# Attention in a hybrid block: adding the two row halves of a head's output by DMA in DRAM, one low part of k for both heads, and a 65th column in the sum of squares

## The chip, the cores and the metric

The kernel runs on one core of one Trainium2 chip. A core has five engines that each work through a queue of their own in order: TensorE (PE, matmuls; the loads of its stationary operand are shown apart as PEld), VectorE (DVE), ScalarE (ACT), GpSimd (POOL) and SyncE (SP, which only issues transfers). DMA transfers are issued here by SP and by POOL; POOL's go through a queue of their own ("software" in the profile), SP's through another ("hardware").

The metric is the device time of one execution in microseconds (us).

## The reference

One layer of a decoder trunk, sequence 1024, model width 1024, all in float32. The change touches the attention group (8 heads of 64).

```python
hn = rms_norm(h, norm1_g[i])
proj = hn @ w_in[i]
...
q = rms_norm(q.reshape(bsz, s_len, ATTN_HEADS, HEAD_DIM), q_norm_g[i])
k = rms_norm(k.reshape(bsz, s_len, ATTN_HEADS, HEAD_DIM), k_norm_g[i])
...
y_b = stick_breaking_attention(q, k, v).reshape(bsz, s_len, ATTN_W)
...
h = h + jnp.concatenate([y_a, y_b, y_c], axis=-1) @ w_out[i]
f = jnp.square(jax.nn.relu(rms_norm(h, norm2_g[i]) @ w_ff1[i]))
h = h + f @ w_ff2[i]
gate = jax.nn.sigmoid(rms_norm(h, norm3_g[i]) @ w_ple_gate[i])
h = h + gate * (p[i] @ w_ple_proj[i])
```

```python
def stick_breaking_attention(q, k, v):          # per block of 128 queries
    z = jnp.einsum('bqhd,bkhd->bhqk', qi, kj) * scale
    causal = s_pos < t_pos
    log_beta = jax.nn.log_sigmoid(z)
    log_rem = jnp.where(causal, jax.nn.log_sigmoid(-z), 0.0)
    suffix = lax.cumsum(log_rem, axis=3, reverse=True) - log_rem
    weights = jnp.where(causal, jnp.exp(log_beta + suffix), 0.0)
    o = jnp.einsum('bhqk,bkhd->bqhd', weights, vj)
```

## The kernel before

**Precision.** A float32 operand is kept as two rounded parts, hi and lo; a product is three matmuls, hi*hi, hi*lo and lo*hi (`product`, L157 to L163). `split` (L131 to L139) makes the two parts: hi on ACT, lo on DVE.

**The stages.** First the input, its norm and two small projections. Then, from about 60 us, the spatial gating and `project(0)`. Then the attention of four pairs of heads: `attend(pr)` is woven on PE with `project(pr + 1)`, which makes q, k and v of the next pair; beside `attend(3)` stands `convolve` (`weave`, a count of units of work decides whose turn it is). Then the output projection w_out, the squared-ReLU MLP (two thirds of the time, done as a seven-product block scheme), and the gate at the end.

**project(pr)** loads eight weight blocks `w_qkv` (`load_w`: an SP transfer into one of 7 `stage` buffers, hi on ACT, lo on DVE, or on POOL for the even ones). For each of eight blocks of 128 tokens, 24 matmuls fill the bank `qkv_ps` (one of two). Then a chain follows: ACT squares q and k into `qk_sq` (L335), DVE sums 64 columns for each of four heads (L337), DVE scales the sums and adds the epsilon, which here depends on the token (`ms1e[t]`, L339), POOL takes the power -1/2 (`rs`, L169), DVE multiplies (L345), and V is split. `turn_qk` transposes two blocks at a time and makes `QS` (q's hi and lo, stacked in the 128 partitions) and `KH` (k's hi twice). k's low part has a tile for each head and half of the sequence: `KL[hh][th]`, whose own 64 partitions DVE writes (L370, two instructions of 64 partitions) and whose other 64 POOL sets to zero (L323).

**attend(pr)** does eight steps, head 0 with g = 0 to 3, head 1 with g = 3 to 0, g a block of 256 queries. `stick` makes z (L402: k's hi against q's hi and lo; L404: k's low part, 128 partitions of which 64 are zero; L408: the mask), two sigmoids on ACT (L409, L410), a scan on DVE (L413) and a product on POOL or DVE (L416). `gather` transposes the weights (`w_tr`), splits them into `wT_hi` and `wT_lo`, and multiplies with V, hi in 64 columns and lo in the other 64, so that the bank `av` holds two row halves whose sum is the output. ACT copies one half to `av_lo` (L462), DVE adds it to the other (L463) into `y_b`, and SP stores `y_b` to `y_dram` once per half of the sequence (L466). `av_lo` and `qk_sq` share one pool of three buffers (`half_tmp`, L79).

**POOL's other work in this stretch** is `block_sums` (L282 to L300): before each `gather` it issues up to two transfers of 1 MB that build sums of blocks of `w_ff2` in DRAM (`w_sums`), by plain copies (L300) and by copies that add to what stands there (L297).

**The order.** The program is written in this order, but a scheduler decides what stands where in each engine's queue. On the chip each queue is worked through in that fixed order.

Of the kernel before, what the change touches and what calls it, by code (L numbers as in the profile page):

```python
# [7 lines left out]
F32 = mybir.dt.float32  # L8
F32R = mybir.dt.float32r
AF = mybir.ActivationFunctionType  # L10
ALU = mybir.AluOpType
AX = mybir.AxisListType

P = 128
# [4 lines left out]
HD = 64  # L19
PLE = 256  # L20
FT = 16
EPS = 1e-6
STAGES = 7
WBUFS = 20
SLOTS = 56
LATE = {"w": 22, "raw": 4, "sum": 6, "tmp": 12, "R": 2}
# [6 lines left out]
def hybrid_block(ctx: ExitStack, tc: tile.TileContext, a: dict):  # L33
# [5 lines left out]
    nc = tc.nc  # L39
# [9 lines left out]
    tp = front.enter_context(tc.tile_pool(name="tp", bufs=6))  # L49
# [7 lines left out]
    def name(s):  # L57
        n_of[0] += 1
        return f"{s}_{n_of[0]}"

    def slot(s, dt=F32, shape=(P, HT)):
        return sp.tile(list(shape), dt, tag="slot", name=name(s))
# [10 lines left out]
    def halves(s, dt=F32, shape=(P, HT)):  # L73
        return [slot(s, dt, shape) for _ in range(2)]
# [1 line left out]
    def tmp(s, dt=F32, shape=(P, HT)):  # L76
        return tp.tile(list(shape), dt, tag="tmp", name=name(s))

    def half_tmp(s, dt=F32):  # L79
        return tp.tile([P, 256], dt, tag="half", name=name(s), bufs=3)  # L80

    def bank(pool, s):
        return pool.tile([P, HT], F32, tag=pool.name, name=name(s))
# [9 lines left out]
    half = [slice(0, HT), slice(HT, T)]  # L93
# [34 lines left out]
    gk = load_const("gk", [P, 1])  # L128


    def split(src, hi, lo, scale=None, low=nc.vector):  # L131

        if scale is None:
            nc.scalar.copy(hi, src)  # L134
            low.tensor_tensor(out=lo, in0=src, in1=hi, op=ALU.subtract)  # L135
        else:
            nc.scalar.activation(hi, src, AF.Copy, scale=scale)
            nc.vector.scalar_tensor_tensor(out=lo, in0=src, scalar=scale, in1=hi,  # L138
                                           op0=ALU.mult, op1=ALU.subtract)  # L139
# [70 lines left out]
    ms1e, r1, r1h = [], [], []  # L210
# [20 lines left out]
    lo_p, hi_p = slice(0, HD), slice(HD, P)  # L231
# [72 lines left out]
    y_dram = dram.tile([6, 2, P, HT], F32, name="y_dram")  # L304

    def project(pr):

        wk = [load_w(a["w_qkv"][pr, k], 384, nc.gpsimd if pr and k % 2 == 0 else nc.vector)
              for k in range(KT)]

        QS = [[None, None], [None, None]]

        KH = [[None, None], [None, None]]
        KL = [[None, None], [None, None]]
        V = [None] * 4
        low_q = [None, None]
        heads[pr] = QS, KH, KL, V, low_q
        for t in range(KT):
            th, ts = block(t)
            if t % 4 == 0:  # L320
                for hh, other in enumerate((hi_p, lo_p)):
                    KL[hh][th] = slot("KL", F32R)
                    nc.gpsimd.memset(KL[hh][th][other].bitcast(F32), 0.0)  # L323
                KH[0][th] = slot("KH", F32R)
                QS[0][th] = slot("QS", F32R)
                low_q[th] = slot("q_lo", F32R)
                QS[1][th] = slot("QS", F32R)
                KH[1][th] = slot("KH", F32R)
            ps = bank(ps_mm, "qkv_ps")[:, :384]
            for k0 in range(0, KT, 2):  # L330
                product(ps, [(cols(xn[k][th], ts), wk[k]) for k in (k0, k0 + 1)],
                        k0 == 0, k0 == KT - 2)
                yield 18
            sq = half_tmp("qk_sq")
            nc.scalar.activation(sq, ps[:, :256], AF.Square)  # L335
            ss = small.tile([P, 4], F32, tag="ss", name=name("ss"))
            nc.vector.tensor_reduce(out=ss, in_=sq.rearrange("p (h d) -> p h d", d=HD),  # L337
                                    axis=AX.X, op=ALU.add)
            nc.vector.tensor_scalar(out=ss, in0=ss, scalar1=1.0 / HD, scalar2=ms1e[t],  # L339
                                    op0=ALU.mult, op1=ALU.add)  # L340
            rs = small.tile([P, 4], F32, tag="rs", name=name("rs"))
            power_mhalf(rs, ss, 4)
            if t % 2 == 0:
                qk = tp.tile([P, 2, 256], F32, tag="qk", name=name("qk"), bufs=2)
            nc.vector.tensor_tensor(  # L345
                out=qk[:, t % 2].rearrange("p (h d) -> p h d", d=HD),
                in0=ps[:, :256].rearrange("p (h d) -> p h d", d=HD),
                in1=rs.unsqueeze(2).broadcast_to([P, 4, HD]), op=ALU.mult)
            if t % 2 == 0:
                V[t // 2] = slot("V", F32R, (P, 2, 2, 2, HD))  # L350
            v = V[t // 2][:, t % 2]
            split(ps[:, 256:].rearrange("p (h d) -> p h d", d=HD), v[:, :, 0], v[:, :, 1], scale=r1[t])
            if t % 2 == 1:
                later(72, lambda t=t, qk=qk: turn_qk(heads[pr], t, qk))

    def turn_qk(head, t, qk):

        QS, KH, KL, _, low_q = head
        th = t // 4
        tr = bank(ps_tr, "qk_tr")  # L360
        for i in range(2):
            for j in range(2):
                o = j * 256 + i * P
                nc.tensor.transpose(tr[:, o:o + P], qk[:, i, j * P:(j + 1) * P], ident)
        ws = slice((t % 4 - 1) * P, (t % 4 + 1) * P)

        split(tr[:, :256], QS[0][th][:, ws], low_q[th][:, ws], scale=gq)
        nc.scalar.activation(KH[0][th][:, ws], tr[:, 256:], AF.Copy, scale=gk)
        for hh, own in enumerate((lo_p, hi_p)):
            nc.vector.scalar_tensor_tensor(out=KL[hh][th][own, ws], in0=tr[own, 256:],  # L370
                                           scalar=gk[own], in1=KH[0][th][own, ws],
                                           op0=ALU.mult, op1=ALU.subtract)
        if t % 4 == 3:
            nc.scalar.copy(KH[1][th][hi_p], KH[0][th][hi_p])
            nc.scalar.copy(KH[1][th][lo_p], KH[0][th][hi_p])
            nc.scalar.copy(KH[0][th][hi_p], KH[0][th][lo_p])
            nc.vector.tensor_copy(QS[1][th][hi_p], QS[0][th][hi_p])
            nc.vector.tensor_copy(QS[1][th][lo_p], low_q[th][hi_p])
            nc.vector.tensor_copy(QS[0][th][hi_p], low_q[th][lo_p])
        return 8  # L380
# [3 lines left out]
    def attend(pr):  # L384

        QS, KH, KL, V, _ = heads[pr]
        yb = halves("y_b")
        weights = {}

        def stick(hh, g):  # L390
            weights[hh, g] = []
            for t in (2 * g, 2 * g + 1):
                W = (t + 1) * P
                th, ts = block(t)

                rem = at.tile([P, T], F32, tag="rem", name=name("rem"), bufs=3)
                wt = at.tile([P, T], F32, tag="wt", name=name("wt"), bufs=4)
                for kh in reversed(range(th + 1)):
                    n = min(HT, W - kh * HT)
                    ks = slice(kh * HT, kh * HT + n)  # L400
                    z = bank(ps_z, "z")[:, :n]
                    nc.tensor.matmul(z, QS[hh][th][:, ts], KH[hh][kh][:, :n],  # L402
                                     start=True, stop=False)
                    nc.tensor.matmul(z, QS[hh][th][:, ts], KL[hh][kh][:, :n],  # L404
                                     start=False, stop=kh < th)
                    if kh == th:

                        nc.tensor.matmul(z[:, n - P:], ident_r, below, start=False, stop=True)  # L408
                    nc.scalar.activation(rem[:, ks], z, AF.Sigmoid, scale=-HD ** -0.5)  # L409
                    nc.scalar.activation(wt[:, ks], z, AF.Sigmoid, scale=HD ** -0.5)  # L410

                back = rem[:, :W][:, ::-1]
                nc.vector.tensor_tensor_scan(out=back, data0=back, data1=back, initial=1.0,  # L413
                                             op0=ALU.mult, op1=ALU.bypass)
                on_vector = t in (3, 5, 7)
                done = (nc.vector if on_vector else nc.gpsimd).tensor_tensor(  # L416
                    out=wt[:, :W - 1], in0=wt[:, :W - 1], in1=rem[:, 1:W], op=ALU.mult)
                if not on_vector:
                    last_pool[0] = done
                weights[hh, g].append(wt)  # L420
                yield 2 * (t + 1) + 10

        def gather(hh, g):
# [21 lines left out]
            for j in range(-2, g + 1):  # L445
# [12 lines left out]
                                         stop=kb == 2 * g + 1 and part is lo)  # L458
                yield 8

            low = half_tmp("av_lo")
            nc.scalar.copy(low[:HD], av[HD:])  # L462
            nc.vector.tensor_tensor(out=yb[g // 2][own, (g % 2) * 256:(g % 2 + 1) * 256],  # L463
# [6 lines left out]
        for i, step in enumerate(steps):  # L470
            if i + 1 < len(steps):
                yield from stick(*steps[i + 1])
            block_sums(8 * pr + i, last_pool[0])
            yield from gather(*step)

    ATTEND = 2 * (72 + 8 * 10 + 72 + 10 * 10 + 80)

# [619 lines left out]
```

## Time and profile before

| | |
|---|---|
| median of 3 runs | 1260.59 us (1258.04 to 1261.03) |
| profiled execution | 1262.6 us, of it 1260.9 us from the first to the last instruction (the span) |
| busy: PE, DVE, ACT, POOL | 96%, 70%, 48%, 29% of the span |
| mean granted TensorE clock | 0.984 of full speed |
| transfers: hardware queue, software queue | 168.08 MB, 65.70 MB |

In the rows below a group reads: line, engine, operation, output <- inputs, shapes, count, then busy time and mean duration of one, then the idle time of the engine just before them and who ended it. A timeline row is start, duration, engine, line, operation, tiles and count. A window row has the length of the stretch, then the busy time and the count of instructions for each engine, then the granted clock, the share of the time in which the DMA engines were busy, and GB/s.

### The profile page before, as it was taken

The page shows a single profiled execution, that of the slowest core. Times are in us where ns is not written, and L with a number is a line of the kernel's source. Part 1 is how long each engine was busy: PE and PEld are TensorE (multiplying, and loading weights), DVE is VectorE, ACT ScalarE, POOL GpSimd, SP SyncE. Part 2 cuts the span into 40 slices and gives each one's busy share as a digit, 9 for nine tenths or more (in the row PEclk, how much of TensorE's full clock was granted, in tenths as well). Part 3 has the DMA queues.
Part 4 walks back from the last instruction along what each step waited for, and adds up shares of the span by engine and source line. Part 5 has one row for each costly group of instructions (what it writes and reads, how often), then busy time and mean ns, then how long its engine had stood idle before and what let it go on. Part 6 is the DMA issues. An engine that isn't in the chain of part 4 may idle for free.

```text
span 1260.9 us, 17509 instructions
## 1 busy us (share of the span) xinstructions
PE 1215.0 (96%) x5868; PEld 1034.1 (82%) x5868; DVE 880.7 (70%) x1324; ACT 603.8 (48%) x1167; POOL 364.2 (29%) x365
## 2 busy tenths in 40 slices
PE   9999898899999999879999999999999999999998
PEld 7898798898888878658888888888888888888887
DVE  7746886898979654676887777777755565686443
ACT  7725655666656454553334334344544344555211
POOL 2324434455323212233553453431000000122110
PEclk9999998999999999989999999999999999999999
DMA  9603257788542298689999999958956565653231
GB/s 309 211 18 117 84 158 210 167 210 159 119 114 38 67 292 226 175 221 251 269 244 255 252 244 250 252 193 302 354 179 224 183 223 170 203 166 106 76 111 51
DMA packets 118700, 234.89 MB, mean 186 GB/s; under 512 B 13105, under 2 KB 20529, under 8 KB 118353
## 3 DMA queue, kind: packets, MB, share of 16 engines
q1 hardware_dynamic: 94752, 168.08, 40.4%
q0 software_dynamic: 23856, 65.70, 23.3%
q8 instruction: 46, 0.75, 0.3%
q14 instruction: 46, 0.37, 0.1%
HBM read 176.57 MB, written 78.64 MB: 202 GB/s over the span
## 4 chain that ended last, share of the span: by engine, by line
PE 82%; DVE 8%; DMA 5%; issue 2%; ACT 1%; POOL 1%; SPq 0%; DVEq 0%; POOLq 0%; ACTq 0%
PE d_ps L731 24%; PE f_ps L731 24%; PE qkv_ps L161 3%; PE qkv_ps L162 3%; PE qkv_ps L163 3%; PE g_ps L161 2%; PE g_ps L163 2%; PE g_ps L162 2%; DVE rem L413 2%; PE av L456 2%; DMA S<-sq 2%; PE w_tr L438 1%; PE cv_ps L161 1%; DMA h_dram<-h 1%; PE cv_ps L162 1%
## 5 line engine op out<-in xcount | busy, mean ns | idle before, releaser
L135 DVE TENSOR_TENSOR w_lo<-raw,w_hi 128x512 fp32r<-128x512 f32 x268 | 244.9, 916 | 94.4 <-ACT w_hi L134 92.2
L134 ACT CAST w_hi<-raw 128x512 fp32r<-128x512 f32 x268 | 165.2, 619 | 242.6 <-PE d_ps L731 116.7
L731 PE MATMUL f_ps<-hn_hi,w_hi 128*128 128x512 f32 x448 | 176.5, 394 | 5.3 <-ACT v L884 5.3
L731 PE MATMUL f_ps<-hn_lo,w_hi 128*128 128x512 f32 x448 | 175.7, 392 | 0.0
L731 PE MATMUL f_ps<-hn_hi,w_lo 128*128 128x512 f32 x448 | 175.3, 392 | 0.0
L731 PE MATMUL d_ps<-f_hi,w_lo 128*128 128x512 f32 x448 | 174.3, 389 | 0.0
L731 PE MATMUL d_ps<-f_hi,w_hi 128*128 128x512 f32 x448 | 174.3, 389 | 0.0
L731 PE MATMUL d_ps<-f_lo,w_hi 128*128 128x512 f32 x448 | 174.3, 389 | 0.0
L731 PEld LDWEIGHTS f_ps<-hn_hi,w_hi 128*128 128x128 f32 x448 | 85.1, 190 | 23.4 <-ACT v L884 5.7
L719 POOL TENSOR_TENSOR S<-S,sq 128x512 f32<-128x512 f32 x14 | 22.6, 1614 | 273.5 <-ACT sq L788 273.5
L731 PEld LDWEIGHTS f_ps<-hn_lo,w_hi 128*128 128x128 f32 x448 | 85.1, 190 | 17.9 <-issue 0.2
L731 PEld LDWEIGHTS f_ps<-hn_hi,w_lo 128*128 128x128 f32 x448 | 85.0, 190 | 18.0
L731 PEld LDWEIGHTS d_ps<-f_hi,w_hi 128*128 128x128 f32 x448 | 84.1, 188 | 17.6
L731 PEld LDWEIGHTS d_ps<-f_lo,w_hi 128*128 128x128 f32 x448 | 84.1, 188 | 17.4
L731 PEld LDWEIGHTS d_ps<-f_hi,w_lo 128*128 128x128 f32 x448 | 84.1, 188 | 17.3
L413 DVE TENSOR_TENSOR_SCAN rem<-rem 128x128 f32<-128x128 f32 (+3 forms) x64 | 89.0, 1393 | 11.1 <-ACT rem L409 10.6
L161 PE MATMUL qkv_ps<-whi,xn_hi 128*128 128x384 f32 x256 | 92.0, 359 | 2.6 <-DVE V L138 2.6
L163 PE MATMUL qkv_ps<-whi,xn_lo 128*128 128x384 f32 x256 | 89.8, 351 | 0.0
L162 PE MATMUL qkv_ps<-wlo,xn_hi 128*128 128x384 f32 x256 | 89.8, 351 | 0.0
L135 DVE TENSOR_TENSOR f_lo<-raw,f_hi 128x512 fp32r<-128x512 f32 x112 | 77.6, 723 | 4.6 <-ACT f_hi L134 4.0
L134 ACT CAST f_hi<-raw 128x512 fp32r<-128x512 f32 x112 | 67.0, 620 | 17.9 <-DMA raw<-f_dram 13.4
L416 POOL TENSOR_TENSOR wt<-wt,rem 128x127 f32<-128x127 f32 (+4 forms) x40 | 44.3, 1109 | 107.7 <-DVE rem L413 44.9
(219 smaller groups left out, 2665.7 us busy)
## 6 DMA issues: line engine op xcount, KB each, us to landing
raw<-in_w_ff SPq DMA_DIRECT2D x160, 256.0 KB, 4.1
raw<-f_dram SPq DMA_DIRECT2D x112, 256.0 KB, 4.8
raw<-w_sums SPq DMA_DIRECT2D x64, 256.0 KB, 3.7
f_dram<-f SPq DMA_DIRECT2D x48, 256.0 KB, 4.4
f_dram<-t SPq DMA_DIRECT2D x48, 256.0 KB, 3.9
w_sums<-in_w_ff POOLq DMA_DIRECT2D x8, 1024.0 KB, 11.7
w_sums<-w_sums POOLq DMA_DIRECT2D x8, 1024.0 KB, 12.4
raw<-in_w_ff POOLq DMA_DIRECT2D x32, 256.0 KB, 5.4
```

The lines of the kernel that those rows point to most:

```text
L134: nc.scalar.copy(hi, src)
L135: low.tensor_tensor(out=lo, in0=src, in1=hi, op=ALU.subtract)
L161: nc.tensor.matmul(ps, lh, rh, start=first and i == 0, stop=False)
L162: nc.tensor.matmul(ps, lh, rl, start=False, stop=False)
L163: nc.tensor.matmul(ps, ll, rh, start=False, stop=last and i == len(terms) - 1)
L413: nc.vector.tensor_tensor_scan(out=back, data0=back, data1=back, initial=1.0, op0=ALU.mult, op1=ALU.bypass)
L416: done = (nc.vector if on_vector else nc.gpsimd).tensor_tensor(out=wt[:, :W - 1], in0=wt[:, :W - 1], in1=rem[:, 1:W], op=ALU.mult)
L438: nc.tensor.transpose(tr[:, n:n + P], wts[i][:, kb * P:(kb + 1) * P], ident)
L456: nc.tensor.matmul(av[:, first * P:], lhs, part[:, o:o + m], start=kb == 0 and part is hi, stop=kb == 2 * g + 1 and part is lo)
L719: return eng.tensor_tensor(out=out, in0=x, in1=y, op=ALU.add)
L731: nc.tensor.matmul(bank, l, r, start=first and k == 0 and i == 0, stop=k == len(b) - 1 and i == 2, skip_group_check=True)
```

## The change

Three edits, all in `project` and `attend`.

1. **Output by DMA.** For pairs 0 to 2 ACT copies the whole bank half (128 partitions) into a buffer `both` (its tile is named `av`), SP stores its lower 64 partitions into `y_dram`, and one step later POOL issues a transfer that adds the upper 64 to what stands there (`sum_rows`). The DVE addition, the tile `y_b` and its store are kept for pair 3 alone. The buffer is free again when the adding transfer has landed. The shared pool has four buffers now.
2. **One low part of k.** `KL[th]` holds both heads, written by one DVE instruction of 128 partitions in `split`; POOL's zeroing goes. The matmul on it takes the head's own 64 partitions of `QS` and `KL`, instead of 128.
3. **A 65th column.** `qk_sq` has 65 columns per head; ACT copies `ms1e[t]` into the last and squares with a scale of 1/8, so that DVE's sum is already the scaled one and the instruction of L339 goes.

```diff
+HALVES = 4
...
-    def half_tmp(s, dt=F32):
-        return tp.tile([P, 256], dt, tag="half", name=name(s), bufs=3)
+    def half_tmp(s, shape=(P, 256)):
+        return tp.tile(list(shape), F32, tag="half", name=name(s), bufs=HALVES)
...
             if t % 4 == 0:
-                for hh, other in enumerate((hi_p, lo_p)):
-                    KL[hh][th] = slot("KL", F32R)
-                    nc.gpsimd.memset(KL[hh][th][other].bitcast(F32), 0.0)
+                KL[th] = slot("KL", F32R)
...
-            sq = half_tmp("qk_sq")
-            nc.scalar.activation(sq, ps[:, :256], AF.Square)
+
+            sq = half_tmp("qk_sq", (P, 4, HD + 1))
+            nc.scalar.copy(sq[:, :, HD], ms1e[t].broadcast_to([P, 4]))
+            nc.scalar.activation(sq[:, :, :HD], ps[:, :256].rearrange("p (h d) -> p h d", d=HD),
+                                 AF.Square, scale=HD ** -0.5)
             ss = small.tile([P, 4], F32, tag="ss", name=name("ss"))
-            nc.vector.tensor_reduce(out=ss, in_=sq.rearrange("p (h d) -> p h d", d=HD),
-                                    axis=AX.X, op=ALU.add)
-            nc.vector.tensor_scalar(out=ss, in0=ss, scalar1=1.0 / HD, scalar2=ms1e[t],
-                                    op0=ALU.mult, op1=ALU.add)
+            nc.vector.tensor_reduce(out=ss, in_=sq, axis=AX.X, op=ALU.add)
...
-        nc.scalar.activation(KH[0][th][:, ws], tr[:, 256:], AF.Copy, scale=gk)
-        for hh, own in enumerate((lo_p, hi_p)):
-            nc.vector.scalar_tensor_tensor(out=KL[hh][th][own, ws], in0=tr[own, 256:],
-                                           scalar=gk[own], in1=KH[0][th][own, ws],
-                                           op0=ALU.mult, op1=ALU.subtract)
+        split(tr[:, 256:], KH[0][th][:, ws], KL[th][:, ws], scale=gk)
...
-        yb = halves("y_b")
-        weights = {}
+        yb = halves("y_b") if pr == 3 else None
+        weights, unsummed = {}, []
+
+        def sum_rows():
+
+            while unsummed:
+                to, low = unsummed.pop(0)
+                nc.gpsimd.dma_start(to, low, accum_op=ALU.add)
...
-                    nc.tensor.matmul(z, QS[hh][th][:, ts], KL[hh][kh][:, :n],
+                    own = (lo_p, hi_p)[hh]
+                    nc.tensor.matmul(z, QS[hh][th][own, ts], KL[kh][own, :n],
                                      start=False, stop=kh < th)
...
+            if yb is None:
+                both = half_tmp("av")
+                nc.scalar.copy(both, av)
+                to = y_dram[pr, g // 2, own, (g % 2) * 256:(g % 2 + 1) * 256]
+                nc.sync.dma_start(to, both[:HD])
+                unsummed.append((to, both[HD:]))
+                return
             low = half_tmp("av_lo")
...
             block_sums(8 * pr + i, last_pool[0])
+            sum_rows()
             yield from gather(*step)
+        sum_rows()
```

What that makes of the queues is shown at one place, the end of pair 1's attention, where the weights of `project(3)` are split. POOL's queue there, before (`w_sums` are the 1 MB transfers, `wlo` the low parts of weights, `rs` the power, `wt` the product of L416):

```order
L416 TENSOR_TENSOR wt_3036<-wt_3036,rem_3035 128x127
L169 TENSOR_TENSOR rs_2999<-ss_2996,mhalf 128x4
L416 TENSOR_TENSOR wt_3046<-wt_3046,rem_3045 128x255
L297 DMA w_sums<-in_w_ff 512x512 x2
L297 DMA w_sums<-w_sums 512x512 x2
L135 TENSOR_TENSOR wlo_3115<-stage_3112,whi_3114 128x384
L323 MEMSET KL_3148 64x512
L323 MEMSET KL_3150 64x512
L135 TENSOR_TENSOR wlo_3127<-stage_3124,whi_3126 128x384
L135 TENSOR_TENSOR wlo_3139<-stage_3136,whi_3138 128x384
L416 TENSOR_TENSOR wt_3214<-wt_3214,rem_3213 128x127
L169 TENSOR_TENSOR rs_3095<-ss_3092,mhalf 128x4
```

And after (the lines of the changed kernel stand 1 to 11 higher; L389 is the new adding transfer):

```order
L170 TENSOR_TENSOR rs_2977<-ss_2975,mhalf 128x4
L136 TENSOR_TENSOR wlo_3093<-stage_3090,whi_3092 128x384
L136 TENSOR_TENSOR wlo_3105<-stage_3102,whi_3104 128x384
L389 DMA y_dram<-av_2899 64x256
L418 TENSOR_TENSOR wt_3013<-wt_3013,rem_3012 128x127
L418 TENSOR_TENSOR wt_3023<-wt_3023,rem_3022 128x255
L298 DMA w_sums<-in_w_ff 512x512 x2
L298 DMA w_sums<-w_sums 512x512 x2
L136 TENSOR_TENSOR wlo_3117<-stage_3114,whi_3116 128x384
L389 DMA y_dram<-av_3009 64x256
L170 TENSOR_TENSOR rs_3073<-ss_3071,mhalf 128x4
```

The four block transfers moved behind two weight splits, and the adding transfer of `av_3009` stands behind all four.

ACT's queue a little later, at block 1 of `project(3)`, before:

```order
L462 COPY av_lo_3302<-av_87 64x256
L137 ACTIVATE V_3274<-qkv_ps_3157,r_566 128x2x64
L335 ACTIVATE qk_sq_3356<-qkv_ps_3277 128x256
L134 CAST wT_hi_3377<-w_tr_3373 128x384
L409 ACTIVATE rem_3305<-z_3307 128x128
L410 ACTIVATE wt_3306<-z_3307 128x128
```

And after (L335 is now the copy into the 65th column):

```order
L465 COPY av_3275<-av_87 128x256
L135 CAST wT_hi_3351<-w_tr_3347 128x384
L335 COPY qk_sq_3330<-ms_564 128x4
L336 ACTIVATE qk_sq_3330<-qkv_ps_3250 128x4x64
L411 ACTIVATE rem_3278<-z_3280 128x128
L412 ACTIVATE wt_3279<-z_3280 128x128
```

The copy into `qk_sq_3330` is new in front of the square, and `qk_sq_3330` lies in the buffer that `av_3009` had, so this copy waits for the adding transfer of `av_3009`; the sigmoids of L411 and L412 stand behind it.

SP's queue at the same place, before:

```order
L66 DMA stage_4031<-in_w_conv 128x384
L466 DMA y_dram<-y_b_2305 128x512
L66 DMA stage_4037<-in_w_conv 128x256
L66 DMA stage_4231<-in_w_conv 128x384
L66 DMA stage_4237<-in_w_conv 128x384
```

And after:

```order
L467 DMA y_dram<-av_2899 64x256
L67 DMA stage_4004<-in_w_conv 128x384
L67 DMA stage_4010<-in_w_conv 128x256
L67 DMA stage_4203<-in_w_conv 128x384
L67 DMA stage_4209<-in_w_conv 128x384
L467 DMA y_dram<-av_3009 64x256
```

The store of the rows of this step (in `y_b_2305` before, `av_3009` now) has moved behind three more weight loads, each of which waits for a `stage` buffer.

More of the change, by code (lines that the diff above doesn't have):

```diff
@@ L313, in project @@
         KH = [[None, None], [None, None]]
-        KL = [[None, None], [None, None]]
+        KL = [None, None]
         V = [None] * 4
```

## The prediction

> **What bounds the kernel now.** I read the page first.
>
> ```profile
> PE 1215.0 (96%) x5868; PEld 1034.1 (82%) x5868; DVE 880.7 (70%) x1324; ACT 603.8 (48%) x1167; POOL 364.2 (29%) x365
> ...
> PE   9999898899999999879999999999999999999998
> ...
> PEclk9999998999999999989999999999999999999999
> ```
>
> PE is the bound almost everywhere, and most of all in the MLP, which the change doesn't touch. So only the slices with an 8 matter, and those of the attention are where the change works. Windows over that stretch, and over the part behind it in which pair 3 runs beside the convolution:
>
> ```profile
> 100.00:365.00 265.00, 240.14 (x1454) 223.66 (x1453) 214.24 (x365) 162.09 (x386) 115.35 (x115) 0.96 0.61 153
> 370.00:440.00 70.00, 70.00 (x388) 60.24 (x386) 57.19 (x75) 35.76 (x75) 19.95 (x15) 1.00 0.21 53
> ```
>
> In the first PE is idle for 265 - 240.1 = 24.9 us, and the granted clock of 0.96 costs 0.04 x 265 = 10.6 us more. That is all that there is to gain. DVE is busy for 214 us of it. In the second PE has no gap at all: nothing that relieves DVE is worth anything there. The chain of waits in the first stretch, by line:
>
> ```profile
> by line: PE qkv_ps L161 11.6%; PE qkv_ps L162 10.9%; PE qkv_ps L163 10.7%; DVE rem L413 10.3%; PE av L456 5.7%; issue 5.0%; DVE wT_lo L135 4.1%; PE w_tr L438 4.0%; DMA stage<-in_w_qkv 3.3%; DVE ss L339 2.5%; DVE KL L370 2.4%; DVE wt L416 2.
> ```
>
> PE and DVE take turns in it, the PE items shown making about 43%, so about half with the rest. DVE instructions that the change removes (L339, L370) are on it.
>
> **The change part by part.** *DVE's relief.* The groups that go, in the first stretch:
>
> ```profile
> L339 DVE TENSOR_SCALAR ss<-ss,ms 128x4 f32<-128x4 f32 x28 | 11.4, 412 | 0.4
> ...
> L370 DVE SCALAR_TENSOR_TENSOR KL<-qk_tr,c_gk,KH 64x256 fp32r<-64x256 f32 x30 | 14.3, 478 | 2.0 <-ACT KH L368 1.7
> ...
> L463 DVE TENSOR_TENSOR y_b<-av,av_lo 64x256 f32<-64x256 f32 x24 | 9.9, 411 | 1.6 <-ACT av_lo L462 1.2
> ...
> L138 DVE SCALAR_TENSOR_TENSOR q_lo<-qk_tr,c_gq,QS 128x256 fp32r<-128x256 f32 x15 | 7.1, 475 | 1.7 <-ACT QS L137 1.7
> ```
>
> L339 goes wholly (11.4 us). L370 goes from two instructions to one; on 128 partitions it costs what q_lo costs, 475 ns, so half goes (7.2 us). L463 goes for pairs 0 to 2 (9.9 us). That is 28.5 us of DVE's 214. Of L339, 2.5% x 265 = 6.6 us lie on the chain, of L370 2.4% x 265 = 6.4 us, of which half goes. That is 58% and 45% of their busy time; L463 at 50% gives 4.9 us. On the chain: 6.6 + 3.2 + 4.9 = 14.7 us. Behind a shortened DVE wait PE's own queue is late next, so I take two thirds: **-10 us**. The ends are 0 and -14.7.
>
> *ACT* makes 24 more small copies here, and `both` is copied at the price of `av_lo` (the partitions are free). The nearest row for a copy of 128x4 is the smallest activation:
>
> ```profile
> L410 ACT ACTIVATE wt<-z 128x128 f32<-128x128 f32 x13 | 3.8, 290 | 6.4 <-PE w_tr L438 6.4
> ```
>
> At most 24 x 0.29 = 7 us; ACT is busy 162 of 265 us and not on the shown chain, so 1 us, between 0 and 4.
>
> *POOL* loses the zeroing and gets 24 adding transfers. The nearest row for those is the sum of squares of the late stage, which is also an adding transfer:
>
> ```profile
> L323 POOL MEMSET KL<- 64x512 f32 x12 | 6.2, 520 | 0.6
> ```
>
> ```profile
> L790 POOL DMA_DIRECT2D S<-sq x14: 843/857/892, 457.7 to 548.1; - x14
> ...
> DMA to landing us min/median/max: 3.4/5.2/8.0
> ```
>
> 24 x 0.86 - 6.2 = +14.4 us on an engine that is busy 115 of 265 us. Behind each stand the power (`rs`) and the product of L416, so a little shows. Each adding transfer also waits until its store by SP has landed; a store is issued a step earlier, except at the place that follows. Together +2 us, between 0 and 6.
>
> *The buffers.* This is the term that decides. `both` and `qk_sq` share four buffers, and `both` is held until its adding transfer lands. That transfer goes through POOL's queue, in which the 1 MB block transfers go too. At the end of pair 1 POOL issues four of them together; the timeline of POOL, and the instructions of L297 between 262 and 272 us:
>
> ```profile
> 265.73 2.18 POOL L297 DMA_DIRECT2D w_sums<-in_w_ff  x2
> 267.11 2.88 POOL L297 DMA_DIRECT2D w_sums<-w_sums  x2
> ...
> 272.24 1.97 POOL L135 TENSOR_TENSOR wlo<-stage,whi 128x384 fp32r<-128x384 f32 x2
> ```
>
> ```profile
> L297 POOL DMA_DIRECT2D w_sums<-in_w_ff x2: 1111/1272/1432, 265.7 to 266.5; - x2
> L297 POOL DMA_DIRECT2D w_sums<-w_sums x2: 1833/2047/2261, 267.1 to 267.7; - x2
> ...
> DMA to landing us min/median/max: 10.7/20.3/28.8
> ```
>
> They were issued within 2 us and landed 10.7 to 28.8 us later: one after the other, the last at 267.7 + 28.8 = 296.5 us. In the new order two weight splits (1.97 us) and one adding transfer (0.86 us) stand ahead of them, so the last lands at about 296.5 + 2.8 = 299.3 us, and `av_3009`, which stands behind all four, at about 300. Its buffer is wanted by the copy into `qk_sq_3330`. Before, that square stood here in ACT's timeline:
>
> ```profile
> 285.34 0.37 ACT L462 COPY av_lo<-av 64x256 f32<-64x256 f32 x1
> ...
> 286.08 0.38 ACT L335 ACTIVATE qk_sq<-qkv_ps 128x256 f32<-128x256 f32 x1
> ...
> 286.70 0.30 ACT L409 ACTIVATE rem<-z 128x128 f32<-128x128 f32 x1
> ```
>
> So ACT stands for about 300 - 286 = 14 us. Both ends shift alike if the stretch before gets shorter. Behind it on ACT are the sigmoids of z, the casts of `wT_hi` and V, so PE's two z banks and its transposes stop. PE can still do one product into the other `qkv_ps` bank (24 matmuls at some 0.18 us, starts in the next fence), 4 us, then it is idle for some 10 us; 2 us more go to a drop of the granted clock, since the stretch lost 10.6 us that way on 24.9 idle ones. **+12 us**. The ends are 0 (the transfer lands in time) and +16.
>
> At the same place the store of `av_3009` waits behind loads that need freed `stage` buffers:
>
> ```profile
> 269.83 7.59 SPq L66 DMA_DIRECT2D stage<-in_w_conv  x7
> ```
>
> So it lands near 279 us, and POOL, waiting for it, holds back one `rs` that ran at 275; that is in POOL's 2 us.
>
> *PE.* The low product takes 64 partitions instead of 128; the number of columns that stream is unchanged, so nothing is gained. What a change of the array's rows between two matmuls costs no row shows. The neighbourhood of a z:
>
> ```profile
> 142.67 0.34 PE L162 MATMUL qkv_ps<-wlo,xn_hi 128*128 128x384 f32 x1
> 142.85 0.39 PE L402 MATMUL z<-KH,QS 128*128 128x512 f32 x1
> 143.08 0.40 PE L404 MATMUL z<-KL,QS 128*128 128x512 f32 x1
> 143.31 0.34 PE L163 MATMUL qkv_ps<-whi,xn_lo 128*128 128x384 f32 x1
> ...
> 144.02 1.03 PE L438 MATMUL w_tr<-ident,wt 128*128 128x128 f32 x8
> 144.81 0.47 PE L402 MATMUL z<-KH,QS 128*128 128x512 f32 x1
> ```
>
> ```profile
> L404 PE MATMUL z<-KL,QS x76: 272/365/479, 106.0 to 355.5; 128*128 128x512 f32 x37, 128*128 128x128 f32 x13, 128*128 128x256 f32 x13, 128*128 128x384 f32 x13
> ```
>
> Matmuls start 0.23 us apart and last 0.39 us, so 0.16 us overlap. If none may overlap across a switch, each low product costs two switches, 0.32 us. The 76 of the first stretch count half (PE's share of the chain): 12.2 us. The 20 others (96 in all) run where PE has no gap: 6.4 us. Upper end +18.6. Lower end 0: z follows transposes, another kind of matmul, 0.24 us before these are over. That is the nearest row, so I take a quarter of the upper end, **+4.6 us**. The Trainium skill, "TensorEngine Tiling (Array Packing)", section "Key Properties", says that changing the tiling mode drains TensorE; by that this term would be the upper end, and no row here shows such a change.
>
> Sum: -10 + 1 + 2 + 12 + 4.6 = +9.6 us. The profiled execution took 1262.6 us, so 1272.2 for such a one; it lies 2.0 above the median of 1260.59, so **1270 us** against that.
>
> **The rivals.** *The buffer comes back in time (faster).* Place: the copy at 286 us. It decides by whether `av_3009` lands before 286, so whether the software queue serves a small transfer beside the four large ones. For it: the small adding transfers of L790 land in 5.2 us. Against it: those have no 1 MB transfers in front, and the four above landed one after the other. Without the 12 us the sum is -2.4, 1258 us; with the switches and POOL's work hidden as well it is -10, 1250.6. I put it at 1254.
>
> *The array drains at each switch.* 18.6 in place of 4.6: 1284 us. For it: the overlap that it would take away is in the rows. Against it: the transposes' row. The rule cited above says this; no row here bears it out or refutes it.
>
> *The waits for buffers come more than once.* At the end of pair 0 the same order stands: block transfers, then an adding transfer (`av_2110`) whose buffer the copy of `av_2376` wants. Before:
>
> ```profile
> 188.92 1.02 POOL L135 TENSOR_TENSOR wlo<-stage,whi 128x384 fp32r<-128x384 f32 x1 [0.58 <-ACT whi L134]
> ```
>
> ```profile
> 212.92 0.37 ACT L462 COPY av_lo<-av 64x256 f32<-64x256 f32 x1
> ```
>
> The two adding block transfers stand now behind that split, two products and an adding transfer, so are issued near 193 us. At some 7 us each (28.8 / 4) they end near 207, and 213 is when the copy wants its buffer. A slip of 6 us eats that margin, and a wait of 8 us makes 1278.
>
> *A short stall.* If the four transfers meet a less busy memory and land 7 us earlier, the stall is half: 1263 us, no change.
>
> **How the numbers follow.** About 0.3% (3.8 us, so 1256.8 to 1264.4) is what a measurement of this kernel can tell from no change. The forecast has 0.42 (its own range 1263 to 1277), the buffer in time 0.22 (0.16 of it faster), the drain 0.16, more waits 0.10, the short stall 0.10 (0.07 of it no change). Of the forecast 0.02 each may fall on faster and on no change. Faster: 0.18. Same: 0.06 + 0.07 + 0.02 = 0.15. Slower: 0.67. The range leaves out the fastest corner of the first rival and the sum of drain and more waits: 1250 to 1287.
>
> **What would show it.** Right: among ACT's waits a new one of some 14 us for `qk_sq` on the transfer of `av` to `y_dram`, near 285 us, and an idle PE right behind it; DVE busy near 850 us (880.7 less about 31 over the kernel); POOL near 376 (364.2 + 24 x 0.86 - 16 x 0.52). Starts of L404's matmuls and their followers about 0.27 us apart would confirm the quarter, 0.4 the drain. Wrong: no such wait, or more PE idle time spread over pairs 0 to 2, or a PE that fills DVE's 28 us fully.

## The result, and the profile after

The changed kernel takes 1273.7 us (median of 4 runs, 1269.04 to 1275.14) against 1260.63 us of the kernel before (median of 4 runs): ratio 1.011, 95% interval 1.009 to 1.0131. So it is slower by 11 to 17 us. The forecast was 1270 in a range of 1250 to 1287. The executions that were profiled lie closer together than the medians: 1269.0 us after and 1262.6 us before.

The page of the kernel after, its busy time of each engine, and the by-line part of its chain of waits:

```profile
PE 1238.9 (98%) x5868; PEld 1028.8 (81%) x5868; DVE 858.1 (68%) x1252; ACT 606.4 (48%) x1199; POOL 375.0 (30%) x373
...
PE d_ps L742 24%; PE f_ps L742 21%; PE qkv_ps L162 3%; PE qkv_ps L163 3%; PE qkv_ps L164 3%; DMA y_dram<-av 3%; PE av L458 2%; PE g_ps L162 2%; PE g_ps L163 2%; PE g_ps L164 2%; PE z L406 2%; PE w_tr L440 2%; DMA raw<-in_w_ff 2%; PE cv_ps L162 1%; PE cv_ps L164 1%
```

DVE lost 22.6 us and POOL gained 10.8, in the direction that the edits say. But PE, which has the same number of matmuls as before, is busy 23.9 us longer. And transfers of `av` to `y_dram`, which the kernel before doesn't have, make 3% of the chain.

The windows over the attention of pairs 0 to 2 (100 to 365 us) and over the part beside the convolution (columns: window, busy time and instructions of PE, PEld, DVE, ACT, POOL, granted clock, DMA share, GB/s):

```profile
100.00:365.00 265.00, 254.10 (x1431) 217.01 (x1430) 190.94 (x292) 162.09 (x406) 126.92 (x125) 0.97 0.65 158
370.00:440.00 70.00, 70.00 (x360) 54.12 (x359) 52.42 (x66) 36.59 (x79) 17.37 (x13) 1.00 0.16 38
```

In the first window PE's idle time fell from 24.9 to 10.9 us. Still PE finished 23 matmuls fewer in it (1431 for 1454). In the second PE is without a gap in both kernels, at full clock, and does 360 matmuls where it did 388. So the matmuls there got dearer on the mean; that is no wait. (With the same queues but full rows, a1 below, it does 382.)

The waits, from 80 to 450 us, by who waits for whom (total, times, longest):

```profile
ACT qk_sq L335 <- DMA y_dram<-av: 9.8, 1, 9.8
```

```profile
PE z L403 <- ACT wt L412: 5.4, 1, 5.4
```

```profile
POOL y_dram L389 <- DMA y_dram<-av: 32.5, 8, 6.7
```

The first is the forecast stall. The chain of waits between 180 and 310 us has its transfer, which ends at 268.0 + 23.6 = 291.6 us:

```profile
268.02 23.55 DMA y_dram<-av
```

The 3% of the chain are this transfer and one more, at the end of pair 0:

```profile
195.83 13.14 DMA y_dram<-av
```

This one is a store by SP. POOL stands 5.5 us until it has landed, then issues the adding transfer and, behind it, a power (`rs`) that the next V needs. PE waits 1.9 us for that V, at 212.8; before, the wait of this kind at the same place was 1.0 us. So a wait of POOL was on the chain, but it cost PE little.

ACT's timeline around the end of the first one, at 291.6 us, and behind that PE's:

```profile
281.31 0.50 ACT L135 CAST wT_hi<-w_tr 128x384 fp32r<-128x384 f32 x1
291.59 0.20 ACT L335 COPY qk_sq<-ms 128x4 f32<-128x4 f32 x1 [9.78 <-DMA y_dram<-av]
```

```profile
286.70 0.33 PE L164 MATMUL qkv_ps<-whi,xn_lo 128*128 128x384 f32 x1
292.45 0.58 PE L403 MATMUL z<-KH,QS 128*128 128x256 f32 x1 [5.42 <-ACT wt L412]
...
295.38 0.79 PE L406 MATMUL z<-KL,QS 64*128 64x512 f32 x1
```

PE went on for 5 us after ACT stopped, then it stood for 5.4 us. Behind that even a low product of 512 columns takes 0.79 us instead of 0.50: the granted clock has fallen. The windows of after, then of before, over this place:

```profile
270.00:320.00 50.00, 44.44 (x228) 36.05 (x227) 29.26 (x42) 26.95 (x69) 21.64 (x21) 0.90 0.74 136
```

```profile
270.00:320.00 50.00, 44.82 (x288) 41.24 (x286) 44.45 (x67) 34.05 (x81) 27.30 (x24) 1.00 0.94 182
```

The clock of 0.90 costs 5 us of the 50. The gap and the clock together are 5.4 + 5 = 10.4 us, an estimate from this trace. In the same 50 us PE did 60 matmuls fewer than before (228 for 288), and part of that is due to the dearer low products.

And the neighbourhood of a low product in PE's timeline of after, with the weight loads of the same place:

```profile
141.00 0.40 PE L403 MATMUL z<-KH,QS 128*128 128x512 f32 x1
141.33 0.50 PE L406 MATMUL z<-KL,QS 64*128 64x512 f32 x1
141.76 0.44 PE L164 MATMUL qkv_ps<-whi,xn_lo 128*128 128x384 f32 x1
142.03 0.33 PE L162 MATMUL qkv_ps<-whi,xn_hi 128*128 128x384 f32 x1
```

```profile
140.83 0.19 PEld L403 LDWEIGHTS z<-KH,QS 128*128 128x128 f32 x1
141.32 0.18 PEld L406 LDWEIGHTS z<-KL,QS 64*128 64x128 f32 x1 [0.31 <-issue]
141.75 0.19 PEld L164 LDWEIGHTS qkv_ps<-whi,xn_lo 128*128 128x128 f32 x1 [0.25 <-issue]
141.86 0.19 PEld L162 LDWEIGHTS qkv_ps<-whi,xn_hi 128*128 128x128 f32 x1
```

Before, the starts at such a place lay 0.23 and 0.23 us apart (142.85, 143.08, 143.31); now they lie 0.33 and 0.43 apart. The weights of L403 were loaded at 140.83, one matmul ahead of their use. Those of L406 (64 rows), and those of the full-row matmul behind it, begin to load only when their own matmul starts. So at each change of rows the load no longer runs ahead, and the start comes later: by 0.10 us for the low product and by 0.20 for the matmul behind it. That the late load is the reason is argued, not shown; d1 below has a case where 0.10 us is lost though the load was ahead.

### The profile page after: what moved, and what is told of

Its sections match the earlier page's. It is cut to its first block, busy times and chain, and to the rows that moved or that the text cites. A ratio compares the mean times of both kernels' runs of the same rounds, so it can differ in the third digit from the quotient of the medians.

```text
span 1267.3 us, 17566 instructions
## 1 busy us (share of the span) xinstructions
PE 1238.9 (98%) x5868; PEld 1028.8 (81%) x5868; DVE 858.1 (68%) x1252; ACT 606.4 (48%) x1199; POOL 375.0 (30%) x373
## 4 chain that ended last, share of the span: by engine, by line
PE 82%; DMA 8%; issue 5%; DVE 2%; POOL 2%; ACT 1%; SPq 0%; POOLq 0%; DVEq 0%; ACTq 0%
PE d_ps L742 24%; PE f_ps L742 21%; PE qkv_ps L162 3%; PE qkv_ps L163 3%; PE qkv_ps L164 3%; DMA y_dram<-av 3%; PE av L458 2%; PE g_ps L162 2%; PE g_ps L163 2%; PE g_ps L164 2%; PE z L406 2%; PE w_tr L440 2%; DMA raw<-in_w_ff 2%; PE cv_ps L162 1%; PE cv_ps L164 1%
## 5 line engine op out<-in xcount | busy, mean ns | idle before, releaser
L136 DVE TENSOR_TENSOR w_lo<-raw,w_hi 128x512 fp32r<-128x512 f32 x268 | 241.4, 903 | 95.0 <-ACT w_hi L135 94.7
L411 ACT ACTIVATE rem<-z 128x128 f32<-128x128 f32 (+3 forms) x96 | 47.8, 498 | 52.5 <-PE z L410 29.9
```

## The experiments

Each was timed against the kernel before on its own chip; the medians of before there were 1258.0 to 1258.8 us. Theory A was the prediction's own list of terms, theory B that the changes of rows are the larger term.

| kernel | what it is | us | ratio [95%] |
|---|---|---|---|
| a1_full_rows | after, low product on 128 partitions | 1249.65 | 0.9926 [0.9904, 0.9948] |
| a2_own_buffers | after, `av` copied into buffers of its own | 1260.62 | 1.0022 [1.0007, 1.0038] |
| a3_rows_buffers | both | 1249.05 | 0.9921 [0.9899, 0.9942] |
| b1_half_rows | before, low product on 64 partitions | 1279.13 | 1.0161 [1.0138, 1.0185] |
| c1_column | before with the 65th column | 1247.53 | 0.9907 [0.9885, 0.9929] |
| c2_one_low | before with one lo for k, 128 partitions | 1248.45 | 0.9917 [0.9896, 0.9938] |
| c3_dma_out | before with the additions by DMA | 1264.0 | 1.0043 [1.0026, 1.006] |
| a6_rows_no_dma | c1 and c2 together | 1244.28 | 0.9884 [0.9859, 0.9909] |
| e3_column_held | c1, every queue in the order of before | 1250.0 | 0.9926 [0.9905, 0.9947] |
| e4_before_new_order | before, every queue in the order of c1 | 1249.57 | 0.9918 [0.9896, 0.9941] |
| e5_both_held | a6, every queue in the order of before | 1247.24 | 0.9907 [0.9878, 0.9936] |
| d1_both_half | b1, the product ahead on 64 rows too | 1258.12 | 0.9991 [0.9975, 1.0008] |

**The rows: a1 and b1.** Their queues stand word for word in the order of after and of before, but for the rows of one matmul, so nothing but the rows differs.

```diff
 a1, against after
-                    own = (lo_p, hi_p)[hh]
-                    nc.tensor.matmul(z, QS[hh][th][own, ts], KL[kh][own, :n],
+                    nc.tensor.matmul(z, QS[hh][th][:, ts], KL[kh][:, :n],
 b1, against before
-                    nc.tensor.matmul(z, QS[hh][th][:, ts], KL[hh][kh][:, :n],
+                    own = (lo_p, hi_p)[hh]
+                    nc.tensor.matmul(z, QS[hh][th][own, ts], KL[hh][kh][own, :n],
```

> The changed kernel, but the low product of k takes all 128 partitions again, on the tile that holds both heads. (The other head's 64 rows then add the product of two low parts, which is of the order of the rounding of float32.) Theory A, the prediction's terms: the switch between 128 and 64 rows costs 4.6 us and the wait for the buffer 12, so about 1273.7 - 4.6 = 1269 us, with ACT's wait for the adding transfer still there. Theory B, from the trace of after: in the starts of the matmuls each low product costs some 0.28 us more than before (0.09 ahead of it, 0.19 behind it), 96 times, 25 us of PE time, and the gain by DVE's relief is larger than forecast and hidden under it: 1249 to 1256 us, faster than before.

> The kernel before, with only the matmul of k's low part on the head's own 64 partitions instead of 128 (the tiles, their zeroing and the rest as before). It prices the switch of rows alone. Theory A: +4.6, 1265 us. Theory B: 25 us of PE time, of which PE's 24.9 idle us in the attention stretch hide a part: 1272 to 1282 us, and starts of the low products and their followers as far apart as in the changed kernel.

Putting the 64 rows into before costs 0.0161 (20 us). Taking them out of after brings 1.011 - 0.9926 = 0.0184 (23 us). PE's timeline of a1 at the same kind of place, and then of b1:

```profile
141.67 0.40 PE L403 MATMUL z<-KH,QS 128*128 128x512 f32 x1
141.91 0.39 PE L405 MATMUL z<-KL,QS 128*128 128x512 f32 x1
142.13 0.34 PE L164 MATMUL qkv_ps<-whi,xn_lo 128*128 128x384 f32 x1
```

```profile
142.81 0.39 PE L402 MATMUL z<-KH,QS 128*128 128x512 f32 x1
143.13 0.50 PE L405 MATMUL z<-KL,QS 64*128 64x512 f32 x1
143.56 0.44 PE L161 MATMUL qkv_ps<-whi,xn_hi 128*128 128x384 f32 x1
```

The distances are 0.24 and 0.22 us in a1, and 0.32 and 0.43 in b1. Over all 96 low products, start to start and less 0.45 ns per column (what full-row neighbours take), without the waits, b1 has some 26 us of PE time more than before, and after some 26 us more than a1. Theory B holds: this is the largest cost in the change, and 20 to 23 of the 26 us reach the end in these two pairs.

**The buffers: a2 and a3.**

```diff
-                both = half_tmp("av")
+                both = slot("av")[:, :256]
```

> The changed kernel with the copy of av in a buffer of the large pool of slots instead of one of the four that it shares with the squares, so that no square waits for an adding transfer. Theory A (the wait is the largest term): 1273.7 - 12 = 1262 us. Theory B (the switches are the largest): ACT waits 9.8 us in the trace of after, of which PE idles 5.4 and loses some 3 to the granted clock, so 1264 to 1268 us.

> Both at once: 128 partitions for the low product, and the copies of av in the large pool. What is left of the change is DVE's relief, less what POOL's transfers cost. Theory A: 1273.7 - 4.6 - 12 = 1257 us. Theory B: 1242 to 1250 us.

In both, ACT's wait on the transfer is gone. Against after, a2 gains 1.011 - 1.0022 = 0.0088, 11 us, which agrees with the 10.4 us read above. But a3 gains nothing measurable over a1, though a1 still has the stall, the same wait for the same transfer:

```profile
ACT qk_sq L335 <- DMA y_dram<-av: 10.2, 1, 10.2
```

```profile
PE z L403 <- ACT wt L411: 6.5, 1, 6.5
```

One thing stands against reading these as prices of the stall: the other buffers made the scheduler put all queues into another order (counted in the traces, 5460 of PE's 5868 matmuls stand in the same sequence in a2 as in after). What such a reordering is worth, e4 shows below. The stall's 10.4 us are therefore read in the trace; as a price they are not settled by these two runs.

a2 and a3 are a third pair for the rows: their queues stand in one and the same order, and nothing but the rows of the low product differs. Here the rows cost 1.0022 - 0.9921 = 0.0101, 13 us, not 20 to 23. The windows over pairs 0 to 2 of a2, then of a3:

```profile
100.00:365.00 265.00, 257.83 (x1460) 220.49 (x1458) 198.18 (x301) 166.90 (x412) 131.49 (x127) 0.99 0.66 162
100.00:365.00 265.00, 247.00 (x1514) 231.06 (x1513) 202.89 (x308) 168.63 (x425) 130.36 (x130) 0.97 0.67 163
```

With the 64 rows PE is idle for 10.8 us less (7.2 for 18.0), as in the other two pairs (9.1 and 11.3 less). But here the granted clock is also higher, 0.99 for 0.97, some 5 us of 265; in the other two pairs it is not. So how much of the 26 us reaches the end depends on the order around them.

**One edit at a time: c1, c2, c3, a6.** Each is before with one part of the diff (c2 and a6 with the low product on 128 partitions; what this adds to z is the product of two low parts told at a1, so c2's expectation describes it wrongly).

> The kernel before with the 65th column alone (edit 3): k's lo for each head as before, its output added on VectorE as before, three buffers. Theory A (the prediction's terms): two thirds of the 6.6 us that L339's instructions have on the chain, -4.4, and +0.5 for 32 more small ACT copies: some -4 us, 0.997. Theory B (a switch of rows costs more, and the relief of DVE comes through whole or better): -6.6 us, 0.995. Theory C (PE's own queue is late next at each of these places, so a relief spread over a kernel is worth little): -1 us or less. In each, DVE's busy time falls by about 13 us.

> The kernel before with k's lo made once for both heads alone (edit 2), the low product on all 128 partitions (it then also adds the other head's low part times the zero half of that head's q, nothing that changes the sum beyond rounding). No switch of rows, no zeroing on POOL. Theory A: two thirds of the 3.2 us on the chain, -2.1, and -1 for the zeroing: -3 us, 0.998. Theory B: -5 us, 0.996. Theory C: -1 us or less. In each, DVE's busy time falls by about 7.5 us and POOL's by 8.

> The kernel before with the output's row halves added by DMA alone (edit 1), with four buffers. Theory A: -3.3 for the additions, +0.5 for ACT, +3 for POOL, +12 for the wait of qk_sq at the end of pair 1: some +12 us, 1.01, with an ACT wait of 10 to 14 us on the transfer of av near 286 us. Theory B (the wait is worth what it is only because the switches leave PE no work made ahead): an ACT wait of about 10 us is there again, but the time is within 3 us of the kernel before. Theory C: the addition on DVE was beside other work, and the wait is paid whole: +14 us or more.

> Edits 2 (low product on all 128 partitions) and 3 together, the output added on VectorE as before, three buffers. Compared with a1_full_rows and a3_rows_buffers (1249 us), which have the DMA output as well. Theory A: -3 and -4: some 1252 us, and the DMA output with its own buffers is worth another -1 to -3. Theory B: -11 us, 1248: the relief of edits 2 and 3 is the whole gain and the DMA output is worth about nothing. Theory C (the gain of a1 and a3 comes from the DMA output): 1256 or more.

Theory A fails for c1 and c2: 12 and 10 us gained, where it gave 4 and 3. Even theory B had given less (6.6 and 5). Together in a6 they bring 15 us, less than their sum of 22. The additions by DMA lose 5 us alone: more than B gave them, less than A. Next to a1 and a3, a6 is some 5 us faster (0.9884 against 0.9926 and 0.9921, intervals that overlap). So no comparison here shows a gain from the addition by DMA, and alone it is slower. c3's waits, of ACT and then of PE:

```profile
ACT qk_sq L337 <- DMA y_dram<-av: 15.4, 2, 11.9
```

```profile
PE z L410 <- ACT wT_hi L135: 11.8, 1, 11.8
```

Read like the stall of after, this would be 20 us: 11.8 of idle PE and a clock of 0.83 over the 50 us from 270 to 320. The kernel is 5 us slower than before, with the additions gone from DVE. So an estimate of this kind can be well above what reaches the end.

**The order of the queues: e3, e4, e5.** The scheduler re-sorts all queues when one instruction goes or is added: of PE's 5868 matmuls, 5545 stand in the same sequence in c1 as in before. So c1's gain could come from the relief or from the order. These kernels hold every queue in a list of places, written out from the other kernel:

```diff
     with tile.TileContext(nc, schedule_with_timeline_sim=True) as tc:
         hybrid_block(tc, a)
+        hold(tc)
...
+        queue = [line[engine][p] for p in places]
+        for first, then in zip(queue, queue[1:]):
+            tc.add_manual_dep(then, first.name, info, reason="hold")
```

> The program of c1_column (the 65th column alone), but every engine's queue held in the order that the kernel before has: the 32 additions of the mean are gone from DVE, each small copy stands right ahead of its square on ACT, nothing else moves. Theory R (what c1 gained is DVE's relief): as c1, some -10 us, 1248. Theory O (a good part of c1's gain is the new order that the scheduler made of all queues, and the relief itself is near the prediction's term): -3 to -5 us, 1254.

> The program of the kernel before, with the same work, but every engine's queue held in the order that c1_column has; the additions of the mean (L339) stand right behind their sums on DVE. Theory R: no gain from an order alone, 1258, within 3 us of the kernel before. Theory O: -5 to -8 us, 1251.

> Edits 2 (low product on all 128 partitions; it adds q's low part times the low part of k of the other head, a term of the order of float32 rounding) and 3 as in a6_rows_no_dma, but every queue held in the order of the kernel before; a zeroing of two columns of k's lo on POOL stays where the zeroing was. DVE has 20.8 us less to do than before, in the old order. Theory R: as a6, -13 us, 1245. Theory O: the prediction's terms, -4.4 and -2.1 and +0.5: -6 us, 1252.

e3 and e5 came out by theory R, e4 by theory O. The relief in the old order (e3) brings 9 us. The new order with the old work (e4) also brings 10 us, with nothing removed; which part of the order does it is not shown. The two together (c1) bring 12: they remove much of the same idle time (c1's PE is idle for 18.3 us from 100 to 365 us). The windows over pairs 0 to 2 of e3, e4 and e5:

```profile
100.00:365.00 265.00, 245.44 (x1508) 228.77 (x1506) 214.61 (x347) 172.26 (x429) 117.31 (x118) 0.97 0.62 157
```

```profile
100.00:365.00 265.00, 244.81 (x1489) 227.71 (x1488) 218.28 (x371) 168.92 (x399) 116.26 (x117) 0.97 0.61 156
```

```profile
100.00:365.00 265.00, 246.46 (x1524) 229.13 (x1523) 212.29 (x337) 173.56 (x432) 114.50 (x113) 0.99 0.62 157
```

and the busy times of the whole span of the same three:

```profile
PE 1209.6 (97%) x5868; PEld 1029.1 (82%) x5868; DVE 873.3 (70%) x1292; ACT 606.6 (48%) x1199; POOL 362.6 (29%) x365
```

```profile
PE 1208.9 (97%) x5868; PEld 1029.7 (82%) x5868; DVE 871.4 (70%) x1324; ACT 604.5 (48%) x1167; POOL 362.6 (29%) x365
```

```profile
PE 1206.7 (97%) x5868; PEld 1027.9 (83%) x5868; DVE 866.7 (70%) x1276; ACT 606.3 (49%) x1199; POOL 357.1 (29%) x357
```

PE's idle time in the window is 19.6, 20.2 and 18.5 us, where before had 24.9: it falls by 5.3, 4.7 and 6.4. Besides, PE's busy time over the span is 5.4, 6.1 and 8.3 us below the 1215.0 of before, with the same matmuls: with less idle time the granted clock rises (0.96 before, 0.97 to 0.99 here). These are single executions: e5's was the fastest of its six, so its trace lies 18.9 us below that of before, where the medians lie 12 apart.

**Per change or per matmul: d1.**

```diff
-                    nc.tensor.matmul(z, QS[hh][th][:, ts], KH[hh][kh][:, :n],
+                    nc.tensor.matmul(z, QS[hh][th][own, ts], KH[hh][kh][own, :n],
```

> b1_half_rows (the kernel before, its order unchanged, the low product on 64 partitions), with the product ahead of it on the same 64 partitions too; this leaves out q's low part times k's high part. Twice as many matmuls on 64 partitions, but as many switches of rows. If each switch costs: as b1, 1279, within 3 us, the two halves 0.28 us apart at 512 columns or less and the next full product 0.43 us behind. If each matmul on half of the rows costs: +20 us more, 1299.

d1 has 192 products on 64 rows, mostly in pairs, b1 has 96. Worked out from the starts as above, d1 pays 27 us of PE time over before and b1 26. So a pair of products on 64 rows costs what a single one costs: PE pays for each stretch on half of the rows, and not for each matmul in it. But the time does not lie where the expectation put it (0.28 us between the two halves, 0.43 behind):

```profile
144.09 0.50 PE L403 MATMUL z<-KH,QS 64*128 64x512 f32 x1
144.43 0.38 PE L405 MATMUL z<-KL,QS 64*128 64x512 f32 x1
144.75 0.44 PE L439 MATMUL w_tr<-ident,wt 128*128 128x128 f32 x2
```

The distances are 0.34 and 0.32 us: 0.10 is lost between two products on the same rows, though the weights of the second began to load at 144.20, and only 0.09 behind the pair. Why is open.

The time of 1258 us fits neither expectation. Dropping the rows made the scheduler re-sort PE's queue once more (5433 of 5868 matmuls in b1's sequence), and PE is nearly without a gap:

```profile
100.00:365.00 265.00, 263.40 (x1494) 222.63 (x1493) 221.57 (x373) 170.51 (x401) 116.31 (x117) 0.99 0.62 156
```

It is idle there for 1.6 us. That the order alone is behind the 21 us between b1 and d1 is argued from e4 and not shown: no run held d1 in b1's order.

## Why the prediction came out, step by step

The sign and the range were right, and the stall was found. That the value of 1270 lies near 1273.7 is luck: two terms that were both too small stood against each other.

- **The buffer wait, +12.** Mechanism and place were right. ACT waits for the buffer of `qk_sq` until `av`'s adding transfer lands. The wait is 9.8 us, not 14, because both ends lie earlier than forecast: the transfer lands at 291.6, not 300, and the square would have stood at 281.8, not 286. The forecast of 10 us of idle PE and 2 of clock measured 5.4 and 5, together 10.4. So the sum is near, but both of its parts were off, in opposite directions. As a price it stays open: without this wait the kernel gained 11 us on 64 rows (a2 against after) and nothing measurable on 128 (a3 against a1), each time in another order.
- **The change of rows, +4.6.** This is the step that failed: "I take a quarter of the upper end." The runs showed +20 us (b1), +23 us (a1) and +13 us (a2 against a3). Of the two signs that were named, 0.27 and 0.4 us, the trace has 0.33 to 0.43. The row it was leaned on, a transpose ahead of z, changes no rows and could say nothing of it. The upper end of 18.6 had the price per product about right: it allowed 0.32 us per low product, and 0.30 is what a product of 512 columns pays (not as two equal parts, but 0.10 ahead of it and 0.20 behind). It fell short of 20 because it counted the 76 of the first stretch at half.
- The Trainium skill, "TensorEngine Tiling (Array Packing)", section "Key Properties", says that changing the tiling mode drains TensorE. The trace agrees in that such a change costs time, 0.10 us ahead of a 64-row product and 0.20 us behind it; that the array runs empty there, no run here shows.
- **DVE's relief, -10.** Too small. For edits 2 and 3 it came to two thirds of 6.6 + 3.2, 6.5 us of idle time, and e5, which has them alone in the old order, lost 6.4 in the window, though 10.6 over the whole span (e3, with the 65th column alone, lost 5.3 in the window where two thirds of 6.6 are 4.4). That part came out nearly. What failed is what it was made into: the time of e5 fell by 12 us, because PE's busy time fell by 8.3 in its trace as well; the mean granted clock rose from 0.984 to 0.989 over the span, which is some 6 of these. The prediction had quoted 10.6 us lost to the clock on 24.9 us of idle time, and used that for the stall, but not for the relief.
- **What was not in the list: the order.** e4 shows that an order of the queues is worth 10 us by itself. After is a new order too. Its sum is therefore not to be split cleanly. Without the rows, but with the stall (a1, in the order of after), the change brings -9 us, where the prediction's other terms add up to +5; without both (a3, in another order) it brings -10, where they add up to -7.
- **ACT's +1** was not measured alone. ACT's busy time rose by 2.6 us (606.4 for 603.8).
- **POOL's +2** was not measured alone. The prediction let POOL wait for a store at one place; it waits 32.5 us, at eight places. One of these is on the chain of waits, at 196 to 209 us, where PE then waits 1.9 us; how much of the rest reaches the end is open. Its busy time, 375.0, is as forecast (376); DVE's is 858.1 for 850.
- **"The waits come more than once"** did not happen in after: ACT has one such wait. c3 has two.

## The version that beats both

a6_rows_no_dma, 1244.28 us, 0.9884 [0.9859, 0.9909] of before: k's lo made once for both heads with the low product left on all 128 partitions, the 65th column, and the output added on DVE as before. Its lead over c1 (1247.53), a1 and a3 lies within the intervals.

## What to carry to other kernels

Halving the rows of one matmul among full ones saved nothing here and cost two changes of rows, 0.30 us for each such matmul; multiply by the zeros, or by the other head's rows, if the result allows it. Where a scheduler sorts the queues, an edit's time holds its reordering too: hold the order when you want the price of the edit, and look at the order when you want the time. And where the granted clock falls behind idle time, count more than the idle time for a wait: here 24.9 us of it stood beside 10.6 us lost to the clock, and the one gap of 5.4 us beside 5.

## What the runs showed of the hardware

- A weight load runs one matmul ahead of its use between matmuls of the same rows, and at a change of rows it begins only with its own matmul, in after and b1 at all 96 low products. There 0.10 us goes in front of a single 64-row product and 0.20 us behind it, also where no other engine is waited for. A pair of them costs as much in all, 0.09 to 0.10 us in front, between and behind (d1).
- Around a 5.4 us gap of PE (287.0 to 292.5) the granted clock was 0.80 on the mean from 285 to 310 us, and behind it full-row matmuls of 384 columns at 0.52 us for 0.34:

```profile
285.00:310.00 25.00, 19.58 (x87) 15.19 (x85) 11.63 (x16) 11.21 (x28) 10.28 (x8) 0.80 0.37 60
```

- A transfer of 64 KB in POOL's queue, issued at 268.0 us behind four of 1 MB, landed at 291.6, just behind the last of them (266.3 + 24.9 = 291.2) and not beside them. The four land one after the other (274.4, 281.2, 286.5 and 291.2), and three more small ones, issued at 278.7 to 287.4, behind them (291.9, 292.3 and 292.6). The instructions of L298 of after between 255 and 300 us:

```profile
L298 POOL DMA_DIRECT2D w_sums<-in_w_ff x2: 1381/1574/1767, 264.3 to 265.0; - x2
L298 POOL DMA_DIRECT2D w_sums<-w_sums x2: 2172/2373/2574, 265.7 to 266.3; - x2
...
DMA to landing us min/median/max: 10.1/18.5/24.9
```
